# A Griffin-style layer on one core: the output projection in pairs of column groups, with seven block products for eight in some chunks

## The chip, the core and the metric

The kernel runs on one core of a Trainium2 chip. The core has a matrix engine (TensorE, PE in the profile, its weight loads PEld), a vector engine (VectorE, DVE), a scalar engine (ScalarE, ACT), GpSimd (POOL) and a queue engine (SyncE, SP) from which nearly all transfers are issued. Matmuls accumulate in PSUM, which has eight banks of 128 x 512 float32; everything else lies in SBUF. Each engine works through its own queue in order and waits on semaphores for the others. The metric is the device time of one execution in microseconds; less is better.

## The reference

One layer (DEPTH = 1), 256 tokens, width 2048, all in float32:

```python
h = rmsnorm(x, norm_mix_g);  u = h @ w_in          # 12,288 columns
# short-conv branch -> ya, recurrent branch (HGRN2, 8 heads) -> yb
m = sigmoid(ga) * (ya @ w_a_out) + sigmoid(gb) * (yb @ w_b_out)
x = x + m @ w_o                                      # the output projection
gate = sigmoid(rmsnorm(x, ple_norm_g) @ w_ple_gate)
x = x + gate * (p @ w_ple_proj)
return rmsnorm(x, final_norm_g)
```

The output projection is a product of 256 x 2048 by 2048 x 2048. Its result, added to x, is what the gate projection reads after it.

## The kernel before

**Products.** A float32 operand is split into a high part `hi`, rounded to the type that TensorE takes at full rate, and a low part `lo`, the remainder. Each product is three matmuls: hi x hi, hi x lo, lo x hi (`product`, L1097 to L1102). Activations lie transposed in SBUF, 16 row tiles k of 128 features by 256 tokens (two token halves t); they are the stationary operand, and the weights stream past in rows of 512 columns.

**Steps.** All weights pass in one list of 316 steps. A step is a chunk of 256 weight rows by 512 columns: two row tiles, two token halves, three matmuls, so twelve matmuls of 512 columns. A column group of a 2048-row matrix has eight chunks. The groups in order: the small projection PP (4), sixteen groups of the branches, the merge gates ga and gb with A (`w_a`) and B (`w_b`) for each of four column groups, four groups O (`w_o`) and four groups PG (`w_ple_gate`).

**Weights.** `load` (L103) brings two chunks, 1 MB, into one of three `raw` buffers. `split` (L130) writes hi on ScalarE (L151) and lo on VectorE (L152) into one of four `whi`/`wlo` pairs; some steps take theirs from another pool instead, among them the pool `late` from the start of PG, which takes over the memory of the pool `m`. Before each step the main loop splits ahead by three steps and more (`ahead`, L1093), so a split waits until TensorE has finished the step that held its buffer.

**Gate pairs.** For column groups 1 to 3 the gates ga and gb are computed together ("GG"). In four of the eight chunks the eight block products (2 token halves x 2 row tiles x 2 gates) are replaced by seven (the Strassen-Winograd form); the list `PAIR` gives the order of joined units ("S") and plain units of two chunks. A joined unit has four parts with 6, 3, 6 and 6 matmuls. It needs sums of weight blocks, made by VectorE in `combine_weights` (L163, L166, L167), and sums of activation blocks, made once by `forms` (L739 to L747). The products 1, 5, 6, 7 gather in four banks "s", the rest in four banks "g", and `ep_pair` (L754) puts them together on VectorE (L761).

**Epilogues.** What follows a group is a generator (`ep_...`). The main loop resumes every active one after each step, behind the splits of that step. `turned` (L283) transposes a block of 128 x 1024: four transfers of 128 KB out to DRAM (L292), one of 512 KB back in (L294), and a transposition of 32 x 32 blocks on VectorE (L298). The order on each engine's queue is then set by a scheduler, which keeps the dependencies.

**Around the change.** `ep_bb` makes a slice of m, turns it and stores its parts (L810, L811). `ep_o`, once per O group, adds the PSUM banks to x (L821), copies the sum (L822) into a tile that is turned, squares it (L829), and stores the transposed, scaled block as `x1T` (`put`, L256 and L257). Block j becomes the row tiles 4j to 4j+3 of x1T, which every PG group reads from k = 0 to 15 in chunks 0 to 7: block 0 for chunks 0 and 1, block 1 for 2 and 3, block 2 for 4 and 5, block 3 for 6 and 7. `third_part` opens the pool of the last stages and loads the first residual columns, `residual` the others, `load_gfin` the final gain.

Of the kernel before, what the change touches and what calls it, by code (L numbers as in the profile page):

```python
# [15 lines left out]
P = 128  # L16
# [7 lines left out]
CW = 512  # L24
# [17 lines left out]
PAIR = ("S", 0), (0, 2), ("S", 1), (1, 2), ("S", 4), (0, 6), ("S", 5), (1, 6)  # L42
PAIRED = [c for u, c in PAIR if u == "S"]

# [7 lines left out]
def hybrid_kernel(ctx, tc, xT, x, pT, prm, gfin, masks, w_in, w_a, w_b, w_o, w_pg, w_pp, out):  # L52
# [77 lines left out]
    def split(pos, c0=0, c1=2 * CW):  # L130
# [9 lines left out]
        if more(pos) and pos % (4 + MORE) < MORE:  # L140
            pool, n = pools["tmp2"], MORE
# [17 lines left out]
    def combine_weights(pos):  # L159

        b = load(pos).rearrange("p i (k c) -> p (i k) c", k=2)
        t2 = half[unit_of[pos]] = pools["tmp2"].tile([P, CW], F32, tag="t2", bufs=2, name=nm("t2"))
# [8 lines left out]
    for n, (kind, j) in enumerate(IN_ORDER):  # L171
        if j == 0 or kind not in ("ga", "gb"):
            groups.append((kind, j, w_in, n, "hT"))
        elif kind == "ga":
            groups.append(("GG", j, w_in, n, "hT"))
# [3 lines left out]
    groups += [("O", j, w_o, j, "mT") for j in range(4)]  # L179
# [10 lines left out]
    for gi, (kind, j, w, g, op) in enumerate(groups):  # L190
        if kind != "GG":
# [3 lines left out]
        for n, (u, c) in enumerate(PAIR):  # L195
# [3 lines left out]
    last_group = len(steps) - w_pg.shape[2]  # L199


    LEAD, MORE = 3, 1
    first_pair = min(pos for pos, s in enumerate(joint) if s)
    last_pair = max(pos for pos, s in enumerate(joint) if s)

    def more(pos):

        return first_pair - 12 <= pos <= last_pair + 8
# [511 lines left out]
    def forms():  # L720


        for n in range(0, len(PAIRED), 2):
            raw, f = t4(), t4()
            r = raw.rearrange("p (u k t) -> p u k t", u=2, k=2)
            for u in range(2):
                c = PAIRED[n + u]
                nc.sync.dma_start(out=r[:, u], in_=xT[:, 2 * c : 2 * c + 2, :])
            for u in range(2):
                yield  # L730
                for k in range(2):
                    h = r[:, u, k, :]
                    nc.scalar.activation(
                        out=h, in_=h, func=AF.Identity, scale=gain(PRM_GMIX, 2 * PAIRED[n + u] + k)
                    )
            yield
            a11, a12, a21, a22 = (r[:, :, k, t * P : (t + 1) * P] for t in range(2) for k in range(2))
            s1, s2, s3, s4 = (f[:, i * 2 * P : (i + 1) * 2 * P].rearrange("p (u t) -> p u t", u=2) for i in range(4))
            nc.vector.scalar_tensor_tensor(out=s1, in0=a21, scalar=-1.0, in1=a22, op0=ALU.mult, op1=ALU.subtract)  # L739
            nc.vector.scalar_tensor_tensor(out=s2, in0=s1, scalar=-1.0, in1=a11, op0=ALU.mult, op1=ALU.subtract)  # L740
            yield
            nc.vector.tensor_tensor(out=s3, in0=a11, in1=a21, op=ALU.subtract)
            nc.vector.tensor_tensor(out=s4, in0=a12, in1=s2, op=ALU.subtract)
            yield
            hi, lo = (pools["tmp2"].tile([P, 1024], F32R, tag="S" + x, bufs=2, name=nm("S" + x)) for x in "hl")
            nc.scalar.activation(out=hi, in_=f, func=AF.Copy)
            nc.vector.tensor_tensor(out=lo, in0=f, in1=hi.bitcast(F32), op=ALU.subtract)  # L747
            for u in range(2):
                for i in range(4):
                    s = slice((2 * i + u) * P, (2 * i + u + 1) * P)  # L750
                    state["S", PAIRED[n + u], i] = hi[:, s], lo[:, s]
# [43 lines left out]
    def ep_bb(j, psum):  # L795
# [15 lines left out]
        v = nc.vector.tensor_tensor(out=lo, in0=m, in1=hi.bitcast(F32), op=ALU.subtract)  # L811
        if j == 3:

            state["before"] = [(a.ins, v.ins), ()]

    def ep_o(j, psum):
        xs = state["x"]
        x1 = t4()
        for t in range(NT):
            d = xs[:, t, j * CW : (j + 1) * CW]  # L820
            nc.vector.tensor_tensor(out=d, in0=d, in1=psum[t], op=ALU.add)  # L821
            nc.scalar.activation(out=spread(x1, t), in_=blocks(d), func=AF.Copy)  # L822
# [119 lines left out]
    def ep_last(t, halves):  # L942
# [10 lines left out]
        "ga": ep_ga, "gb": ep_gb, "A": ep_a, "B": ep_bb, "O": ep_o, "PG": ep_pg, "PP": ep_pp,  # L953
# [139 lines left out]
    def ahead(pos):  # L1093

        return LEAD + min(max(pos - (last_group - 20), 0) // 4, 5) + MORE * (first_pair - 8 <= pos <= last_pair + 8 - MORE)
# [16 lines left out]
    def pair_products(at):  # L1112

        n, part = at
        u, c = PAIR[n]
# [3 lines left out]
        def add(name, xh, xl, s):  # L1119
            k = left[name]  # L1120
# [6 lines left out]
        def tile_of(k, t):  # L1127
            return (x[:, k, t * P : (t + 1) * P] for x in state["hT"])
# [8 lines left out]
        elif part == 1:  # L1137
            add(6, *state["S", c, 1], a)
        elif part == 2:
            add(5, *state["S", c, 0], a)  # L1140
            add((1, 0), *tile_of(2 * c + 1, 1), b)
        else:
            add((0, 1), *state["S", c, 3], a)
            add(7, *state["S", c, 2], b)
# [4 lines left out]
    plain = [4 * sum(u == i for u, _ in PAIR) for i in range(2)]  # L1149
    total = {(t, g): plain[g] + len(PAIRED) * ((t, g) != (1, 1)) for g in range(2) for t in range(NT)}  # L1150
    total.update({n: len(PAIRED) for n in (1, 5, 6, 7)})

    psum = None
    for pos, (gi, c) in enumerate(steps[:last_group]):
        kind, j, w, g, opname = groups[gi]
# [35 lines left out]
        if kind == "GG":  # L1191
            if c == (0, 0):
                left = dict(total)
                banks = {n: bank("g" if type(n) is tuple else "s") for n in total}
# [157 lines left out]
```

## Time and profile before

| what | value |
|---|---|
| time, median of 3 runs | 817.54 us (817.17 to 819.13) |
| profiled execution, its time | 816.79 us |
| its span, first to last instruction | 815.0 us |
| granted TensorE clock, mean | 0.996 |
| TensorE busy | 804.8 us (99%), 4199 matmuls recorded |
| VectorE busy | 603.9 us (74%) |
| ScalarE busy | 455.8 us (56%) |
| weight loads of w_o | 16 of 1 MB, 5.7 us each from issue to landing |

In the profile's rows of groups, `out<-in` are the program's tile names without buffer numbers, then the shape, the count, the busy time and the mean of one in ns; after the second bar stands the idle time of the engine just before them and what ended it. A timeline row is start, duration, engine, line, operation, and in brackets the idle time before it with its releaser. A row of windows gives, for one stretch, its length and then PE, PEld, DVE, ACT and POOL busy with their instruction counts, the granted clock, the DMA share and GB/s. A row of the chain of waits is start, duration and what the end of the program depended on then. Line numbers are those of the kernel before.

### The profile page before, as it was taken

The numbers are of one execution on the slowest core, as the hardware profiler recorded it, in microseconds if no ns is written. First come the engines' busy times: TensorE is split into PE (matmuls) and PEld (weight loads), VectorE is DVE, ScalarE is ACT, GpSimd is POOL, SyncE is SP. The second block draws the span as 40 slices with busy tenths as digits, with TensorE's granted clock in tenths as the row PEclk, the third lists the DMA queues.
The fourth block names the chain that finished last, engine by engine and source line by source line (L and its number), as shares of the span: only waits on it lengthen the run. The fifth ranks groups of instructions, "written<-read, shape, count | busy, mean of one in ns | idle before, by whom it ended". The sixth has DMA issues, their size and how long they took to land.

```text
span 815.0 us, 10926 instructions
## 1 busy us (share of the span) xinstructions
PE 804.8 (99%) x4199; PEld 668.8 (82%) x4200; DVE 603.9 (74%) x711; ACT 455.8 (56%) x596; POOL 91.1 (11%) x75
## 2 busy tenths in 40 slices
PE   9999999999999999999999999999999999999996
PEld 7888888888888888888888888888888888888885
DVE  6746697967766498967768998998996656679734
ACT  7666465555565465465664565554564455567522
POOL 1000045400000055200001001000100000001210
PEclk9999999999999999999999999999999999999998
DMA  9969655647767555748764774774765788887702
GB/s 341 375 267 335 231 176 205 232 158 240 255 236 249 201 178 191 225 153 262 265 232 155 236 278 142 226 272 144 252 256 170 260 296 298 285 285 280 296 1 104
DMA packets 45556, 188.32 MB, mean 231 GB/s; under 512 B 5184, under 2 KB 14656, under 8 KB 29888
## 3 DMA queue, kind: packets, MB, share of 16 engines
q1 hardware_dynamic: 45360, 187.36, 66.1%
q8 instruction: 33, 0.54, 0.3%
q10 hardware_dynamic: 144, 0.26, 0.1%
q14 instruction: 19, 0.16, 0.1%
HBM read 173.97 MB, written 13.63 MB: 230 GB/s over the span
## 4 chain that ended last, share of the span: by engine, by line
PE 93%; DVE 3%; issue 1%; DMA 1%; ACT 1%; ACTq 0%; POOLq 0%; POOL 0%
PE g L1102 80%; PE g L1122 7%; PE s L1122 3%; DVE wlo L152 2%; ACT whi L151 1%; PE s L1102 1%; PE s L448 1%; DMA raw<-in_w_a 1%; DMA raw<-in_w_pp 1%; DVE raw L163 0%; DVE t L166 0%; PE s L581 0%; PE s L604 0%; PE s L605 0%; PE s L603 0%
## 5 line engine op out<-in xcount | busy, mean ns | idle before, releaser
L152 DVE TENSOR_TENSOR wlo<-raw,whi 128x1024 fp32r<-128x1024 f32 (+1 forms) x307 | 382.5, 1262 | 168.4 <-ACT whi L151 165.3
L151 ACT ACTIVATE whi<-raw 128x1024 fp32r<-128x1024 f32 (+1 forms) x307 | 317.1, 1049 | 254.1 <-PE g L1102 205.7
L1102 PE MATMUL g<-wlo,xh 128*128 128x512 f32 (+1 forms) x720 | 276.7, 384 | 0.0
L1102 PE MATMUL g<-whi,xl 128*128 128x512 f32 (+1 forms) x720 | 276.7, 384 | 0.0
L1102 PE MATMUL g<-whi,xh 128*128 128x512 f32 (+1 forms) x720 | 276.3, 385 | 0.0
L1102 PEld LDWEIGHTS g<-whi,xl 128*128 128x128 f32 x720 | 135.3, 188 | 27.0
L1102 PEld LDWEIGHTS g<-wlo,xh 128*128 128x128 f32 x720 | 135.3, 188 | 26.8
L1102 PEld LDWEIGHTS g<-whi,xh 128*128 128x128 f32 x720 | 135.3, 188 | 26.6
L1102 PE MATMUL g<-whi,mh 128*128 128x512 f32 x128 | 49.8, 389 | 0.0
L1102 PE MATMUL g<-wlo,mh 128*128 128x512 f32 x128 | 49.8, 389 | 0.0
L1102 PE MATMUL g<-whi,ml 128*128 128x512 f32 x128 | 49.6, 389 | 0.0
L1122 PE MATMUL g<-whi,xh 128*128 128x512 f32 x120 | 46.7, 389 | 0.0
L1122 PE MATMUL g<-wlo,xh 128*128 128x512 f32 x120 | 46.7, 389 | 0.0
L1122 PE MATMUL g<-whi,xl 128*128 128x512 f32 x120 | 46.7, 389 | 0.0
L151 ACT ACTIVATE whi<-t 128x512 fp32r<-128x512 f32 x12 | 7.6, 634 | 49.5 <-DVE t L166 49.5
L804 POOL TENSOR_TENSOR t<-ga,gb 128x512 f32<-128x512 f32 x6 | 10.6, 1786 | 193.6 <-issue 118.7
L1102 PE MATMUL g<-whi,yaTh 128*128 128x512 f32 (+1 forms) x74 | 28.0, 389 | 1.1 <-ACT whi L151 0.9
L1102 PEld LDWEIGHTS g<-whi,mh 128*128 128x128 f32 x128 | 24.0, 188 | 5.0
L1102 PEld LDWEIGHTS g<-whi,ml 128*128 128x128 f32 x128 | 24.0, 188 | 5.0
L1102 PEld LDWEIGHTS g<-wlo,mh 128*128 128x128 f32 x128 | 24.0, 188 | 4.9
L502 POOL TENSOR_TENSOR t<-b 128x512 f32<-128x512 f32 x10 | 20.3, 2034 | 68.5 <-DMA t<-turn 41.0
L1102 PE MATMUL g<-wlo,yaTh 128*128 128x512 f32 (+1 forms) x74 | 28.0, 384 | 0.0
(202 smaller groups left out, 860.6 us busy)
## 6 DMA issues: line engine op xcount, KB each, us to landing
raw<-in_w_in SPq DMA_DIRECT2D x73, 1024.0 KB, 4.8
raw<-in_w_in SPq DMA_DIRECT2D x34, 512.0 KB, 6.1
raw<-in_w_o SPq DMA_DIRECT2D x16, 1024.0 KB, 5.7
raw<-in_w_pg SPq DMA_DIRECT2D x16, 1024.0 KB, 5.3
turn<-t SPq DMA_DIRECT2D x72, 128.0 KB, 2.6
t<-turn SPq DMA_DIRECT2D x18, 512.0 KB, 5.2
raw<-in_w_a SPq DMA_DIRECT2D x8, 1024.0 KB, 5.2
raw<-in_w_b SPq DMA_DIRECT2D x8, 1024.0 KB, 6.4
```

The source lines that it names most:

```text
L151: a = nc.scalar.activation(out=hi[:, s], in_=src[:, s], func=AF.Copy)
L152: v = nc.vector.tensor_tensor(out=lo[:, s], in0=src[:, s], in1=hi[:, s].bitcast(F32), op=ALU.subtract)
L448: nc.tensor.matmul(heads(bk)[r, h, c if at is None else slice(at, at + 32)], key(h)[:, r], query(h)[:, c], start=True, stop=True, tile_pos ...
L502: nc.gpsimd.tensor_tensor(out=er, in0=br, in1=ref, op=ALU.subtract)
L804: (nc.vector if j == 3 else nc.gpsimd).tensor_tensor(out=spread(m, t), in0=blocks(ga[:, s]), in1=blocks(gb[:, s]), op=ALU.add)
L1102: nc.tensor.matmul(psum, a, b, start=first and n == 0, stop=last and n == 2)
L1122: nc.tensor.matmul(banks[name], x, y[:, s], start=k == total[name] and i == 0, stop=k == 1 and i == 2)
```

## The change

The four groups O become two pairs "OO", each of two column groups, with the scheme of the gate pairs: here the two halves are two column groups of one matrix. In two of the eight chunks (0 and 1) of each pair seven block products take the place of eight. The sums of activation blocks of m are made once, at the end of `ep_bb` of the first m slice, in the second gate pair. The epilogue `ep_outs` starts when the second joined unit ends: it puts the first column group together, starts its transposition (`turned_out`), and does the second column group after the pair's last step. The lists `OUT0` and `OUT1` give the order of the units. Along with it: the temporary tiles t4 of the gate stage are three instead of four, the weight-sum tile t2 one instead of two, banks are taken at first use, the extra split buffer is also used in the later part of the pairs, and the residual and gain loads stand at other steps.

```diff
+OUT0 = (0, 2), (1, 2), (0, 4), (1, 4), ("S", 0), (0, 6), ("S", 1), (1, 6)
+OUT1 = (0, 2), (1, 2), (0, 4), ("S", 0), (1, 4), (0, 6), ("S", 1), (1, 6)
...
-        bufs = bufs or {"tmp1": 8, "tmp2": 4, "tmp3": 5}[state["tmp"]]
+        bufs = bufs or {"tmp1": 8, "tmp2": 3, "tmp3": 5}[state["tmp"]]
...
-    groups += [("O", j, w_o, j, "mT") for j in range(4)]
+    groups += [("OO", j, w_o, 2 * j, "mT", (OUT0, OUT1)[j]) for j in range(2)]
...
+    gates = range(gates[0] - 12, outs[0])
+    outs = range(outs[0] + 8, outs[-1] + 1)
...
+    def forms(op, pool, tag, r, chunks):
+        f = t4()
+        a11, a12, a21, a22 = (r[:, :, k, t * P : (t + 1) * P] for t in range(2) for k in range(2))
...
+        nc.vector.scalar_tensor_tensor(out=s1, in0=a21, scalar=-1.0, in1=a22, op0=ALU.mult, op1=ALU.subtract)
+        nc.vector.scalar_tensor_tensor(out=s2, in0=s1, scalar=-1.0, in1=a11, op0=ALU.mult, op1=ALU.subtract)
+        yield
+        nc.vector.tensor_tensor(out=s3, in0=a11, in1=a21, op=ALU.subtract)
+        nc.vector.tensor_tensor(out=s4, in0=a12, in1=s2, op=ALU.subtract)
+        yield
...
+        nc.scalar.activation(out=hi, in_=f, func=AF.Copy)
+        nc.vector.tensor_tensor(out=lo, in0=f, in1=hi.bitcast(F32), op=ALU.subtract)
...
+        if j == 0:
+            yield
+            yield from forms("mT", pools["m"], "Sm", m.rearrange("p (u k t) -> p u k t", u=2, k=2), (0, 1))
...
-    def ep_o(j, psum):
+    def ep_outs(p, e, m):
+        xs, g = state["x"], t4()
+        a, b = slice(0, CW), slice(CW, 2 * CW)
...
+        nc.scalar.activation(out=g[:, a], in_=m[1], func=AF.Copy)
+        add(x0, x0, e[0, 0])
+        add(x0, x0, g[:, a])
+        add(g[:, a], g[:, a], m[6])
+        add(g[:, b], g[:, a], m[7])
+        add(x1, x1, e[1, 0])
+        add(x1, x1, g[:, b])
+        first = turned_out(2 * p)
+        next(first)
+        active.append(first)
+        yield
+        add(both, both, m[5].rearrange("p (o c) -> p o c", o=1).to_broadcast([P, 2, CW]))
+        while not state["ended", p]:
+            yield
+        for t in range(NT):
+            add(cols(1)[:, t, :], cols(1)[:, t, :], e[t, 1])
+        add(cols(1), cols(1), both)
+        yield from turned_out(2 * p + 1)
+
+    def turned_out(j):
         xs = state["x"]
         x1 = t4()
         for t in range(NT):
-            d = xs[:, t, j * CW : (j + 1) * CW]
-            nc.vector.tensor_tensor(out=d, in0=d, in1=psum[t], op=ALU.add)
-            nc.scalar.activation(out=spread(x1, t), in_=blocks(d), func=AF.Copy)
+            nc.scalar.activation(out=spread(x1, t), in_=blocks(xs[:, t, j * CW : (j + 1) * CW]), func=AF.Copy)
         turn = turned(x1, 2)
         next(turn)
         yield
...
+            if kind == "OO" and j == 0 and c == (4, 3):
+                residual(1)
+                state["x1T"] = operand(big, "x", KT)
+            if kind == "OO" and j == 1 and c in ((0, 1), (1, 1)):
+                residual(2 + c[0])
+            if kind == "OO" and j == 1 and c == (4, 1):
+                load_gfin()
```

More of the change, by code (lines that the diff above doesn't have):

```diff
@@ L188, in add_step @@
         joint.append(s)
-    for gi, (kind, j, w, g, op) in enumerate(groups):
-        if kind != "GG":
+    for gi, (kind, j, w, g, op, *program) in enumerate(groups):
+        if not program:
             for c in range(w.shape[2]):
@@ L732, in forms @@
                     h = r[:, u, k, :]
-                    nc.scalar.activation(
-                        out=h, in_=h, func=AF.Identity, scale=gain(PRM_GMIX, 2 * PAIRED[n + u] + k)
-                    )
+                    nc.scalar.activation(out=h, in_=h, func=AF.Identity, scale=gain(PRM_GMIX, 2 * chunks[u] + k))
             yield
[L737 to L751, printed above, removed]
+            yield from forms("hT", pools["tmp2"], f"Sx{n}", r, chunks)
             yield
@@ L1093, in ahead @@
     def ahead(pos):
-        return LEAD + min(max(pos - (last_group - 20), 0) // 4, 5) + MORE * (first_pair - 8 <= pos <= last_pair + 8 - MORE)
+        return LEAD + min(max(pos - (last_group - 20), 0) // 4, 5) + MORE * (more(pos + LEAD) is not None and more(pos + LEAD + MORE) == more(pos + LEAD))
     def product(psum, op, k, t, hi, lo, first, last, which=(0, 1, 2)):
@@ L1119, in add @@
         def add(name, xh, xl, s):
+            if name not in banks:
+                banks[name] = bank("g" if type(name) is tuple else "s")
             k = left[name]
```

100 lines of the change are left out of this document (57 added, 43 removed).

## The prediction

> **What bounds the kernel now.** I read the page's engine rows first, then the windows of single stages, then the chain of waits, then timelines around the two stage borders the change touches.
>
> ```profile
> span 815.0 us, 10926 instructions
> PE 804.8 (99%) x4199; PEld 668.8 (82%) x4200; DVE 603.9 (74%) x711; ACT 455.8 (56%) x596; POOL 91.1 (11%) x75
> 506.30:547.10 40.80, 40.80 (x182) 33.78 (x181) 38.23 (x38) 24.03 (x26) 3.53 (x2) 1.00 0.72 252
> 632.00:719.00 87.00, 87.00 (x385) 72.07 (x384) 55.47 (x60) 46.07 (x63) 0.00 (x0) 1.00 0.80 280
> 479.07 5.44 PE g L1122 x24
> ```
>
> TensorE is the bound: in the output projection (third row, 87.00 us) it is busy throughout, and matmuls start every 5.44/24 = 0.2267 us, so a plain chunk step of 12 takes 2.72 us. The paired gate stage before it (506 to 547) already works with seven products; VectorE is there busy 38.23 of 40.80 us. How near VectorE is to the bound there, the chain of waits tells:
>
> ```profile
> 506.50 1.07 ACT whi L151
> 512.71 1.24 DVE raw L163
> 537.12 1.23 DVE wlo L152
> 538.37 5.10 DMA raw<-in_w_a
> 543.58 1.07 ACT whi L151
> 547.63 0.61 DVE ga L761
> 548.28 11.88 PE g L1102 x51
> ```
>
> From 506.50 to 548.24 the chain never touches TensorE: it runs over VectorE's splits and weight sums, through a weight load that a late split released, to the add that frees a PSUM bank, and TensorE's next group waits for that add. TensorE loses almost nothing, but the cushion at 548 is zero: VectorE work added to this stretch comes out at its end in full.
>
> **Removed.** Each pair of column groups has two chunks with seven products of three matmuls instead of eight: 2 x 2 x 3 = 12 matmuls x 0.2267 = 2.72 us of TensorE. All 0.33% of it is on the path. I treat 0.3%, 2.45 us, as what a measurement can tell from no change; the gain alone hardly passes that.
>
> **Added, first place: the forms of m in the second gate pair.** After the first m slice is stored, VectorE builds four sums and one split:
>
> ```profile
> L747 DVE TENSOR_TENSOR Sl<-t,Sh 128x1024 fp32r<-128x1024 f32 x2 | 2.4, 1222 | 0.0
> L739 DVE SCALAR_TENSOR_TENSOR t<-t x2: 421/421/421, 408.8 to 424.8; 128x256 f32<-128x256 f32 x2
> L742 DVE TENSOR_TENSOR t<-t x2: 418/418/419, 408.5 to 426.9; 128x256 f32<-128x256 f32 x2
> 503.62 2.49 DVE L152 TENSOR_TENSOR wlo<-raw,whi 128x1024 fp32r<-128x1024 f32 x2 [0.46 <-ACT whi L151]
> 507.60 5.08 DVE L152 TENSOR_TENSOR wlo<-raw,whi 128x1024 fp32r<-128x1024 f32 x3 [0.30 <-ACT whi L151]
> ```
>
> 2 x 0.42 + 2 x 0.42 + 1.22 = 2.9 us; instructions overlap by nearly 0.1 each, so 2.45. In the changed instruction order they stand inside the first joined chunk, the split ahead of the two multiplications (L799) that end there, so they delay the chain above. VectorE's idle time in that place is 0.46 + 0.30 = 0.76. Delay: 2.45 - 0.76 = 1.7; POOL's addition (L804), which waits for L799, is also pushed onto the next splits, and I take **1.8**. Bounds: 0 (all absorbed) and 2.9. Its ScalarE copy of 1 us is hidden beside VectorE.
>
> **Added, second place: inside the second output pair.** A joined chunk costs VectorE three and a half splits and the weight sums; each pair also gets a longer epilogue:
>
> ```profile
> L152 DVE TENSOR_TENSOR wlo<-raw,whi 128x1024 fp32r<-128x1024 f32 x302 | 379.8, 1273 | 168.2 <-ACT whi L151 165.1 <-PE g L1102 0.9 <-PE s L1102 0.9
> L163 DVE TENSOR_TENSOR raw<-raw 128x1024 f32<-128x1024 f32 x12 | 14.7, 1224 | 0.3
> L166 DVE TENSOR_TENSOR t<-raw 128x512 f32<-128x512 f32 x12 | 8.3, 693 | 0.4
> L821 DVE TENSOR_TENSOR xs<-xs,g 128x512 f32<-128x512 f32 x8 | 5.1, 682 | 0.0
> L761 DVE TENSOR_TENSOR gb<-gb,s 128x1024 f32<-128x1024 f32 x3 | 3.7, 1222 | 0.1
> ```
>
> Joined chunk: 3 x 1.27 + 0.69 + 1.22 + 2 x 0.69 = 7.1 us against 2 x 1.27 = 2.5 for the two steps it replaces: +4.6, four times 18.2. Epilogue: eight adds of 0.68 and two of 1.22 against four of 0.68: +5.2, twice 10.3. VectorE: 55.47 + 28.5 = 84.0 us, about 10% less with the overlaps, in 84.3 us of TensorE. It fits on average; order decides. Let F be the end of the first pair. The second has six plain steps (to F+16.3), a joined chunk (to F+21.1), then unit (1,4). The fourth and third parts of that chunk are split late: ScalarE's queue has the fourth first, its buffer comes free after plain step five, F+13.6; so ScalarE ends at F+15.6, VectorE at F+17.0. Behind it in VectorE's queue stands the transposition of the first output block (1.24 us, row below), then on ScalarE four scalings (1.71), only then the split of unit (1,4): ScalarE F+20.0 to 21.0, VectorE until F+22.2. TensorE wants the low half at F+21.3: wait **0.95**; bounds 0 and 2. The weights of (1,4), issued behind two "turn" transfers at about F+10, land by F+16 and are not late.
>
> **Moved, third place: the start of the gate projection PG.** Before, the third output block was transposed eight steps earlier, and only the fourth came here:
>
> ```profile
> 718.80 1.28 DVE L821 TENSOR_TENSOR xs<-xs,g 128x512 f32<-128x512 f32 x2
> 719.04 0.39 PE L1102 MATMUL g<-whi,xh 128*128 128x512 f32 x1
> 719.01 1.06 ACT L151 ACTIVATE whi<-raw 128x1024 fp32r<-128x1024 f32 x1 [1.38 <-PE g L1102]
> 721.11 0.62 ACT L822 ACTIVATE t<-xs 128x512 f32<-128x512 f32 x1
> 721.75 2.22 SPq L292 DMA_DIRECT2D turn<-t  x4
> 722.25 3.89 ACT L151 ACTIVATE whi<-raw 128x1024 fp32r<-128x1024 f32 x4
> 726.77 0.34 SPq L294 DMA_DIRECT2D t<-turn  x1
> t<-turn SPq DMA_DIRECT2D x18, 512.0 KB, 5.2
> 732.55 1.24 DVE L298 STREAM_TRANSPOSE t<-t 128x1024 f32<-128x1024 f32 x1
> 733.83 1.71 ACT L256 ACTIVATE xh<-t,prm_t 128x256 fp32r<-128x256 f32 x4 [1.50 <-DVE t L298]
> 734.82 1.66 DVE L257 SCALAR_TENSOR_TENSOR xl<-t,prm_t,xh 128x256 fp32r<-128x256 f32 x4
> ```
>
> With E = 719.04, PG's first matmul: copies done at E+2.7, turned out, back in at E+7.7, transposed at E+13.5, first scaled slice about E+15.2 (0.43 a slice). PG needs it at chunk 6, E + 6 x 2.72 = E+16.3: 1.1 us spare, 0.6 for the low part. Now the third block comes here too, and PG reads it at chunk 4, **E+10.9**. Its second copy stands on ScalarE behind the splits of PG chunks 3, 4 and 5. These write the pool that takes over m's memory, so they wait for the last output matmul, as the 719.01 row did (1.38 from PE). Three splits at 3.89/4 and the copy: E + 2.9 + 0.6 = E+3.5. From the end of the copies (721.73) to the first slice (734.26) it took 12.5, of which 0.6 was a transposition held behind a split (726.77 + 5.2 = 731.97, not 732.55): the slice is ready at E+15.4 to E+16.0. TensorE waits 4.5 to 5.1; with the low half **5.1**. Bounds: 2 (copy not held, both transfers quick) and 7. The fourth block's copies, two splits later at E+7.4, cross the third's return on SP, which is issued behind its first two parts; back out about E+12.6, landing E+18, slice E+21; chunk 6 now stands at E+16.3+5.1 = E+21.4: covered, 0.2 at most, taken as nothing.
>
> What such a wait does to the clock, no row shows; the longest wait of the trace, with the granted clock about it:
>
> ```profile
> 5.36 0.50 PE L1102 MATMUL g<-whi,yaTh 128*128 128x256 f32 x2 [0.93 <-ACT whi L151]
> PEclk9999999999999999999999999999999999999998
> ```
>
> After 0.93 us none of the slices that follow shows a lower clock (the last one is the kernel's tail). I take no loss for 5 us either. The Trainium skill, "TensorE: Matmul & The Clock Gate", section "What's actually happening", says that one wholly idle window of about 3.4 us halves the clock until as long a busy one has passed; by it, as an estimate, half of 3.4 us, 1.7 us, would come on top.
>
> **At nothing.** Later sums and bank releases: after F VectorE has one split (1.27), one wide add (1.22) and two adds (0.68 each) queued, so the last bank is free at about F+3.9, while the second unit wants it at F+5.4. The t4 ring of three, the single t2 and the earlier residual and gain loads: the reused buffers were read a unit or more before, and the loads are issued a joined chunk or more before their use. If that cover is gone, a late load costs about one transfer, the 5.2 us above.
>
> **Sum.** -2.72 + 1.8 + 0.95 + 5.1 = +5.1. The profiled execution took 816.79 (span 815.0): 821.9. The median shown, 817.54, lies 0.75 above it: **822.6**.
>
> **Rivals.** (a) The gain stands: transfers land in time, VectorE absorbs the rest. 817.54 - 2.72 = 814.8. For it: a covered fourth block today. Decisive: the third block's slice ready by E+10.9, when its copy would have to end before the last output matmul; its place in the queue, behind three splits that wait for that matmul, speaks against it. (b) Only PG waits, VectorE's delays vanish in lookahead (four to five steps): 817.54 - 2.72 + 5.1 = 819.9. (c) Only the VectorE delays: 817.54 - 2.72 + 2.75 = 817.6, if the splits of PG don't wait. (d) The long wait lowers the granted clock: were it half for as long as the wait, 5.1/2 = 2.5 more, 825.1. By the estimate from the Trainium skill's page it would be 824.3. (e) VectorE, 84.0 of 84.3, becomes the pair stage's bound: without the overlaps and with a second late unit like (1,4) some 3 us more, 825.6.
>
> **How the numbers follow.** All three waits as costed, 0.48 (821 to 824.2, slower); (d) 0.15 slower; (e) 0.06 slower; (b) 0.17, at the bound of 820.0: 0.05 slower, 0.12 same; (c) 0.08 same; (a) 0.06 faster. Slower 0.74, same 0.20, faster 0.06. The likeliest is 822.6. From 817.5 to 826.5 the range takes in (b), (d), (e) and most of (c); it leaves out (a), half of (c) and part of (e), together under 2 in 10.
>
> **What would show it.** 4187 matmuls against 4199 if records are complete; a wait of about 5 us of PE on the third slice (L256's counterpart) four steps into PG, after the copy that stands behind three splits; about 1 us at unit (1,4); the first matmul of the group after the second gate pair some 1.8 us later than the 0.3 of now; the granted clock after the long wait. Wrong it would be by ScalarE copying before E, or by PE waiting nowhere over 1 us.

## The result and the profile after

| | before | after |
|---|---|---|
| median, us | 817.18 (6 runs, 817.03 to 819.13) | 823.40 (6 runs, 822.86 to 823.59) |
| ratio | 1 | 1.0070, 95% interval 1.0057 to 1.0083 |
| profiled execution, us | 816.79 | 823.01 |
| its span, us | 815.0 | 821.1 |
| mean granted clock | 0.996 | 0.995 |

The change makes the kernel slower by 6.2 us, 0.70%. The head of the profile's page after the change:

```profile
span 821.1 us, 10969 instructions
PE 805.7 (98%) x4188; PEld 667.5 (81%) x4188; DVE 631.9 (77%) x748; ACT 462.8 (56%) x607; POOL 88.9 (11%) x75
```

The busy time of TensorE did not fall with its instructions: 11 matmuls fewer are recorded (12 are gone in the program), yet PE is busy 0.9 us longer than the 804.8 before. So some matmuls took longer; the table below has 1.6 us of that at a lower clock, and the rest stands mostly where TensorE starts up or resumes after a wait. VectorE is busy 28.0 us longer (631.9 - 603.9). The waits of TensorE after the change (engine, bank, line, what it waited for: us in total, times, longest):

```profile
PE g L1144 <- ACT xh L261: 3.8, 1, 3.8
PE g L1144 <- DVE ga L770: 0.9, 1, 0.9
...
PE g L1166 <- DVE wlo L153: 0.5, 1, 0.5
PE s L1166 <- DVE wlo L153: 0.3, 1, 0.3
```

L1144 is the plain product (L1102 before), L1166 that of the pairs. The first row is PG's start, the second is that of the third gate group, which waits for an add of the second gate pair, the third belongs to the second output pair and the fourth to the second gate pair. None is over 0.3 us in the kernel before, apart from the kernel's start. The timeline of TensorE at PG's start after the change (start, duration, engine, line, operation, idle time before it):

```profile
729.82 0.39 PE L1144 MATMUL g<-wlo,xh 128*128 128x512 f32 x1
730.04 0.39 PE L1144 MATMUL g<-whi,xl 128*128 128x512 f32 x1
734.26 0.50 PE L1144 MATMUL g<-whi,xh 128*128 128x512 f32 x1 [3.83 <-ACT xh L261]
734.60 0.40 PE L1144 MATMUL g<-wlo,xh 128*128 128x512 f32 x1
734.83 0.44 PE L1144 MATMUL g<-whi,xl 128*128 128x512 f32 x1
735.11 0.56 PE L1144 MATMUL g<-whi,xh 128*128 128x512 f32 x1
735.47 0.63 PE L1144 MATMUL g<-wlo,xh 128*128 128x512 f32 x1
735.89 0.63 PE L1144 MATMUL g<-whi,xl 128*128 128x512 f32 x1
...
738.45 0.46 PE L1144 MATMUL g<-whi,xl 128*128 128x512 f32 x1
738.75 0.39 PE L1144 MATMUL g<-whi,xh 128*128 128x512 f32 x1
```

Read the starts, not the durations: 0.227 us apart up to 730.04, then 4.22 us without a start, then from 735.11 to 738.75 nine steps of 0.40 on average (most 0.426). The row of windows for that stretch gives the length, PE's busy time with its instructions, the granted clock, the DMA share and GB/s:

```profile
735.10:738.50 3.40, 3.40 (x10) 0.51 1.02 411
```

The granted clock is 0.51 for 3.4 us: TensorE is called busy all through and does half the work. The loss is 3.64 - 9 x 0.227 = 1.60 us.

So the 6.1 us between the spans are made up like this, each item by the starts of matmuls less 0.227 a matmul:

| item | us |
|---|---|
| 12 matmuls fewer | -2.72 |
| place 1: 0.60 at 519.1 to 520.1, and 1.22 instead of 0.43 at the third gate group, 549 | +1.4 |
| place 2: unit (1,4), 697.0 to 699.0 | +1.04 |
| place 3: the third block's slice, 730.0 to 734.6 | +4.1 |
| half clock behind it | +1.6 |
| start of the execution (first product at 5.82 us, before 5.36) | +0.46 |
| rest | +0.2 |

The start varies from one execution to the next, whatever the kernel: in the traces of e3, e5, f2 and o1 below, matmuls of 512 columns stand 0.427 us apart until 9.1 to 9.4 us, so that 15 matmuls fall between 5 and 9 us instead of 20 to 22, and the products behind run about 1.5 us late. So the single times of most kernels here lie in two groups some 1.5 to 2.5 us apart, and below stretches inside the trace are compared as well, from the 100th product to the last matmul (779.7 us before, 785.4 after).

The chain of place 3, rows of the timelines of ScalarE, SP and VectorE after the change. The last output matmul starts at 719.16, PG's first, E, at 719.39:

```profile
719.36 2.96 ACT L152 ACTIVATE whi<-raw 128x1024 fp32r<-128x1024 f32 x3
722.23 0.62 ACT L864 ACTIVATE t<-xs 128x512 f32<-128x512 f32 x1
722.87 5.24 SPq L297 DMA_DIRECT2D turn<-t  x6
728.28 0.34 SPq L299 DMA_DIRECT2D t<-turn  x1
732.42 1.25 DVE L303 STREAM_TRANSPOSE t<-t 128x1024 f32<-128x1024 f32 x1 [1.62 <-DMA t<-turn]
733.70 1.71 ACT L261 ACTIVATE xh<-t,prm_t 128x256 fp32r<-128x256 f32 x4 [5.18 <-DVE t L303]
```

Three splits at E, then the second half of the third block's copy, the transfers out, the return at E+8.9 behind the first two transfers of the fourth block (the x6 instead of x4), back in after 4.1 us, transposition, first slice at 734.13 = E+14.7. PG wants it at E+10.9.

### The profile page after: what moved, and what is told of

The parts are those of the page before. It is cut to its first block, busy times and chain, and to the rows that moved or that the text cites. A ratio compares the mean times of both kernels' runs of the same rounds, so it can differ in the third digit from the quotient of the medians.

```text
span 821.1 us, 10969 instructions
## 1 busy us (share of the span) xinstructions
PE 805.7 (98%) x4188; PEld 667.5 (81%) x4188; DVE 631.9 (77%) x748; ACT 462.8 (56%) x607; POOL 88.9 (11%) x75
## 4 chain that ended last, share of the span: by engine, by line
PE 85%; DVE 8%; issue 2%; ACT 2%; DMA 2%; ACTq 0%; SPq 0%; POOLq 0%; POOL 0%; DVEq 0%
PE g L1144 66%; PE g L1166 13%; DVE wlo L153 4%; PE s L1166 3%; ACT whi L152 2%; DVE raw L164 1%; PE s L1144 1%; PE s L453 1%; DMA raw<-in_w_a 1%; DMA raw<-in_w_pp 1%; DVE xs L838 1%; DMA t<-turn 1%; DVE t L303 0%; DVE t L167 0%; ACT xh L261 0%
## 5 line engine op out<-in xcount | busy, mean ns | idle before, releaser
L1144 PE MATMUL g<-whi,xh 128*128 128x512 f32 (+1 forms) x720 | 277.4, 386 | 3.8 <-ACT xh L261 3.8
L1144 PE MATMUL g<-wlo,xh 128*128 128x512 f32 (+1 forms) x720 | 277.5, 385 | 0.0
L1144 PE MATMUL g<-whi,xl 128*128 128x512 f32 (+1 forms) x720 | 277.2, 385 | 0.0
L1144 PEld LDWEIGHTS g<-whi,xh 128*128 128x128 f32 x720 | 135.7, 188 | 31.4 <-ACT xh L261 4.2
L1144 PEld LDWEIGHTS g<-whi,xl 128*128 128x128 f32 x720 | 135.7, 189 | 27.2 <-DVE xl L262 0.2
L1144 PEld LDWEIGHTS g<-wlo,xh 128*128 128x128 f32 x720 | 135.7, 188 | 26.5
L152 ACT ACTIVATE whi<-t 128x512 fp32r<-128x512 f32 x16 | 10.1, 634 | 64.9 <-DVE t L167 64.9
L1166 PE MATMUL g<-wlo,xh 128*128 128x512 f32 x120 | 46.7, 389 | 0.0
L1166 PE MATMUL g<-whi,xl 128*128 128x512 f32 x120 | 46.7, 389 | 0.0
L1166 PE MATMUL g<-whi,xh 128*128 128x512 f32 x120 | 46.7, 389 | 0.0
L1166 PE MATMUL g<-wlo,mh 128*128 128x512 f32 x104 | 40.6, 390 | 0.5 <-DVE wlo L153 0.5
L1166 PE MATMUL g<-whi,ml 128*128 128x512 f32 x104 | 40.5, 389 | 0.0
L1166 PE MATMUL g<-whi,mh 128*128 128x512 f32 x104 | 40.1, 390 | 0.0
L1144 PE MATMUL g<-whi,yaTh 128*128 128x512 f32 (+1 forms) x74 | 28.1, 389 | 1.8 <-DVE ga L770 0.9
L1144 PE MATMUL g<-wlo,yaTh 128*128 128x512 f32 (+1 forms) x74 | 27.9, 384 | 0.0
L1144 PE MATMUL g<-whi,yaTl 128*128 128x512 f32 (+1 forms) x74 | 27.9, 384 | 0.0
L1166 PEld LDWEIGHTS g<-whi,xh 128*128 128x128 f32 x120 | 22.5, 188 | 4.7
L1166 PEld LDWEIGHTS g<-whi,xl 128*128 128x128 f32 x120 | 22.5, 188 | 4.7
```

Source lines behind the costliest of these rows:

```text
L152: a = nc.scalar.activation(out=hi[:, s], in_=src[:, s], func=AF.Copy)
L1144: nc.tensor.matmul(psum, a, b, start=first and n == 0, stop=last and n == 2)
L1166: nc.tensor.matmul(banks[name], x, y[:, s], start=k == total[name] and i == 0, stop=k == 1 and i == 2)
```

## The experiments

All times are medians; the kernel before ran beside every one on the same chip, 817.2 to 817.5.

### Each place by itself

**e3: place 1 alone.** The kernel before, with nothing but the sums of m and the buffers that pay for them:

```diff
-        bufs = bufs or {"tmp1": 8, "tmp2": 4, "tmp3": 5}[state["tmp"]]
+        bufs = bufs or {"tmp1": 8, "tmp2": 3, "tmp3": 5}[state["tmp"]]
...
-        t2 = half[unit_of[pos]] = pools["tmp2"].tile([P, CW], F32, tag="t2", bufs=2, name=nm("t2"))
+        t2 = half[unit_of[pos]] = pools["tmp2"].tile([P, CW], F32, tag="t2", bufs=1, name=nm("t2"))
...
+        if j == 0:
+            yield
...
+            nc.scalar.activation(out=shi, in_=f, func=AF.Copy)
+            nc.vector.tensor_tensor(out=slo, in0=f, in1=shi.bitcast(F32), op=ALU.subtract)
```

> The kernel before with one part of the change: the sums of m for the joined chunks are formed where the changed kernel forms them, in the second gate pair, with their work tile and the two buffers fewer that pay for it, and are used by nothing. Theory (place 1): VectorE and ScalarE are delayed there by the same instructions, and the add that frees a bank before the third gate group comes about 0.8 us later and a split 0.6 us later: 817.2 + 1.4 = 818.6 us. Rival (the loss at 519 and 549 us comes from other edits, as the order of the groups or the pools' buffers): 817.2 us, within 0.3 us, with TensorE's wait before the third gate group at 0.2 us as before.

Measured: 818.69 (11 runs), ratio 1.0016, interval 1.0007 to 1.0025; from the 100th product on 781.2 against 779.7, +1.5. TensorE's waits show the two rows of the changed kernel:

```profile
PE g L1116 <- DVE ga L761: 0.9, 1, 0.9
...
PE s L1136 <- DVE wlo L152: 0.3, 1, 0.3
```

Place 1 is real, comes with the sums of m and the buffers that pay for them, and costs 1.4 to 1.5 us.

**e4: place 1 taken away.** The changed kernel with the sums formed three calls of their generator earlier (the main loop calls it once a step):

```diff
-        m = yield from turned(m, 2 if j == 3 else 19)
+        m = yield from turned(m, {0: 16, 3: 2}.get(j, 19))
```

> The changed kernel with one number other: the first block of m waits for 16 calls before its transposition and not for 19, so that the sums of m are formed earlier than in the last joined chunk of the second gate pair. Theory (place 1 is a matter of where the 2.45 us of VectorE stand): the loss of 1.4 us at 519 and 549 us falls to that of the kernel before, 0.3; 823.4 - 1.4 = 822.0 us, places 2 and 3 as they were. Rival (VectorE is full there wherever they stand): 823.4 us.

Measured: 822.93 (6 runs, 821.23 to 824.31), where 822.0 was expected; ratio 1.0060, interval 1.0044 to 1.0076. The trace is the clearer witness: 784.1 us from the 100th product on instead of 785.4, neither of the two waits of place 1 is left in TensorE's list, and the largest gap between starts there is back to 0.49 us (0.54 before the change, 1.34 in the changed kernel). Places 2 and 3 stand as in the changed kernel. The buffers are still the fewer ones, so the cost hung on where the 2.45 us of VectorE stood, and one number removes it.

**e5: place 2.** One number again, the first block's transposition behind the split of unit (1,4):

```diff
-        turn = turned(x1, 2)
+        turn = turned(x1, 9 if j == 0 else 2)
```

> The changed kernel with one number other: the first block's transposition in the second output pair's place waits for nine calls instead of two, so that the split of unit (1, 4) is issued to VectorE ahead of it. Theory (place 2): TensorE's wait of 0.5 us at 698.6 us and the gaps beside it, 1.04 us in all, go; 823.4 - 1.0 = 822.4 us. Rival (the split is late for its weights or for VectorE's other work there, not for its place in the queue): the wait stays and the time is 823.4 us; a split delayed elsewhere by the transposition in its new place would make it 823.4 us too, with the wait at another unit.

Measured: 826.40, ratio 1.0100, interval 1.0085 to 1.0116: 3.0 us slower than the changed kernel, where 1.0 us less was expected, and from the 100th product on as well (788.4). The wait at 698.6 is gone, and two things come in its place. First, 1.1 us are lost at the next joined chunk (a gap of 0.95 us between starts at 711.35), behind ScalarE's splits:

```profile
709.72 1.06 ACT L152 ACTIVATE whi<-raw 128x1024 fp32r<-128x1024 f32 x1 [3.46 <-PE g L1166]
710.68 0.61 ACT L152 ACTIVATE whi<-t 128x512 fp32r<-128x512 f32 x1
```

The split of the weight sum (`whi<-t`), which in the changed kernel goes first, now stands behind one that waits for TensorE to free its buffer; VectorE has no work for 1.02 us just then and is not what is full. Second, place 3 grows. SP's rows:

```profile
725.14 6.65 SPq L297 DMA_DIRECT2D turn<-t  x6
731.97 0.34 SPq L299 DMA_DIRECT2D t<-turn  x1
```

The third block's return again stands behind two transfers of the fourth block, whose copies now end at 731.0. TensorE waits 6.1 us, and then runs at a granted clock of 0.50 for 5.2 us.

**h1: half of the change.** Only the first two column groups are a pair; the last two are plain groups with the plain epilogue:

```diff
-    groups += [("OO", j, w_o, 2 * j, "mT", (OUT0, OUT1)[j]) for j in range(2)]
+    groups += [("OO", 0, w_o, 0, "mT", OUT0)] + [("O", j, w_o, j, "mT") for j in (2, 3)]
...
```

> Half of the change: only the first two column groups of the output projection are a pair with two joined chunks, the last two are plain groups as before, with the plain epilogue. Theory (the gain is 0.227 us a matmul wherever it is made, and places 2 and 3 belong to the second pair): 6 matmuls fewer, -1.36 us; place 1 stays, since the sums of m are formed at the same point, +1.4; no wait of 0.5 us at a split in the third group and none of 3.8 us in PG, so 817.2 - 1.36 + 1.4 = 817.2 us. Rival (a joined pair costs VectorE and the queues so much that the losses of places 2 and 3 come with each pair): 817.2 - 1.36 + 1.4 and half of the 6.7 us of places 2 and 3 and of the low clock, 820.6 us.

Measured: 817.08 (12 runs), ratio 0.9995, interval 0.9985 to 1.0004, where 817.2 was expected: 6 matmuls won, place 1 lost, nothing at places 2 and 3. The first joined pair carries no price on TensorE beyond place 1; the losses at places 2 and 3 come with the second one.

**h2: the half, and place 1 taken away** (the edits of h1 and e4 together).

> The half of the change with the first pair alone, and the sums of m formed earlier: the first block of m waits for 16 calls before its transposition and not for 19, so that the sums stand in the group before the second gate pair's end and not in its last joined chunk. Theory: place 1 goes, 817.2 - 1.36 = 815.9 us, faster than the kernel before, with TensorE's wait before the third gate group at 0.2 us again. Rival (VectorE is full all through the second gate pair and pays the 2.45 us of the sums wherever they stand): 817.2 us, with the wait at the third gate group near 0.9 us.

Measured: 815.45 (12 runs), ratio 0.9973, interval 0.9964 to 0.9983: faster than before. TensorE's waits hold nothing over 0.3 us but the kernel's start:

```profile
PE s L1028 <- PEq L1405: 0.8, 1, 0.8
PE g L1150 <- ACT whi L152: 0.3, 1, 0.3
PE g L1150 <- DVE ga L770: 0.2, 1, 0.2
```

### The clock

**e2: the wait filled.** Ahead of PG's fifth step (`n` = 16):

```diff
+        if kind == "PG" and j == 0 and c == 4:
+            wb = bank("s")
+            ones = [nc.const_aps.tensor(1.0, [P, i], mybir.dt.bfloat16) for i in (P, CW)]
+            for _ in range(n):
+                tc.keep_in_program_order(nc.tensor.matmul(wb, *ones, start=True, stop=True))
```

> The changed kernel with 16 products of constant tiles, 128x128 by 128x512, ahead of the fifth chunk of PG's first group, into a bank that is then not read: they only fill the wait of 3.8 us on the slice. Theory (the half clock after the wait comes from TensorE's having stood idle for about 4 us): the wait of the fifth chunk's first matmul ends at the same time, since ScalarE ends it, but the matmuls behind it stand 0.227 us apart and not 0.427 us, granted clock 0.99 or more; 823.4 - 1.55 = 821.9 us. Rival (the wide spacing from 735.1 to 738.5 us is the supply of operands after the wait, or belongs to the phase): the spacing stays and the time is 823.4 us.

Measured: 821.38, ratio 1.0054, interval 1.0040 to 1.0067. From the 100th product on it is 784.1 us against 785.4. TensorE resumes at the same moment, and the matmuls behind stand 0.227 us apart:

```profile
730.17 3.67 PE L1273 MATMUL s<-const-bfloat16-1.0 128*128 128x512 bf16 x16
734.26 0.50 PE L1144 MATMUL g<-whi,xh 128*128 128x512 f32 x1 [0.42 <-ACT xh L261]
...
735.34 0.39 PE L1144 MATMUL g<-wlo,xh 128*128 128x512 f32 x1
735.57 0.40 PE L1144 MATMUL g<-whi,xl 128*128 128x512 f32 x1
```

The wide spacing after the wait is the idle time's doing, not the operands'.

**d6: a part of the wait filled** (the same edit, `n` = 6).

> The changed kernel with 6 products of constant tiles in the place where e2 had 16: they fill 1.4 us of the wait of 4.0 us and leave TensorE idle for about 2.6 us in one piece. Theory (what lowers the clock is a stretch in which TensorE does nothing for more than about 3 us; a wait of 1.8 us in f2 did not, those of 4.0 us did): no low clock, matmuls 0.227 us apart after the wait, 823.4 - 1.55 = 821.9 us, as e2. Rival (the clock follows the share of idle time in a longer stretch, and e2 held it only because it filled nearly all of the wait): 0.427 us apart as in the changed kernel for part or all of 3.4 us, 822.6 to 823.4 us.

Measured: 823.85 (4 runs), ratio 1.0076, interval 1.0061 to 1.0092: no gain. My threshold fell:

```profile
730.09 1.48 PE L1273 MATMUL s<-const-bfloat16-1.0 128*128 128x512 bf16 x6
734.17 0.50 PE L1144 MATMUL g<-whi,xh 128*128 128x512 f32 x1 [2.60 <-ACT xh L261]
...
735.45 0.63 PE L1144 MATMUL g<-wlo,xh 128*128 128x512 f32 x1
735.88 0.63 PE L1144 MATMUL g<-whi,xl 128*128 128x512 f32 x1
```

The rival held. 2.60 us without work in one piece were enough, and the half clock (granted 0.50) lasts 3.4 us, as after 3.83 us of idling.

### Place 3: what holds the third block

**f4: its copies ahead of the splits.**

```diff
+            cp = nc.scalar.activation(out=spread(x1, t), in_=blocks(xs[:, t, j * CW : (j + 1) * CW]), func=AF.Copy)
+        if j == 2:
+            state["before"] = [(cp.ins,)]
```

> The changed kernel with one edit: the third block's copies go ahead of the splits of PG that are issued after them; the order of the second output pair and the fourth block stay. Theory (the third block is late for its place behind splits, and when it comes in time the fourth is late next): the wait in PG's fifth step falls from 3.8 to between 1 and 2 us, too short for the low clock, and the fourth block, whose slice was ready 20 us after the last output matmul and is wanted at 16.3 plus that wait, makes up to 2.3 us in the seventh step: 823.4 - 4.1 - 1.55 + 1.5 + 2.3 = 821.5 us. Rival (the copy was ready to go no earlier, because VectorE's sums end only when the splits do): the wait stays at 3.8 us with the low clock behind it, 823.4 us.

Measured: 823.79, ratio 1.0071, interval 1.0058 to 1.0083. That is the rival's time, but not the rival's reason. Rows of ScalarE, SP and VectorE:

```profile
719.55 0.63 ACT L864 ACTIVATE t<-xs 128x512 f32<-128x512 f32 x1 [1.61 <-DVE xs L838]
728.16 1.16 ACT L864 ACTIVATE t<-xs 128x512 f32<-128x512 f32 x2 [2.00 <-DVE xs L838]
730.45 1.99 ACT L152 ACTIVATE whi<-raw 128x1024 fp32r<-128x1024 f32 x2
733.94 1.71 ACT L261 ACTIVATE xh<-t,prm_t 128x256 fp32r<-128x256 f32 x4 [1.50 <-DVE t L303]
...
724.95 0.34 SPq L299 DMA_DIRECT2D t<-turn  x1
...
731.52 1.23 DVE L153 TENSOR_TENSOR wlo<-raw,whi 128x1024 fp32r<-128x1024 f32 x1 [0.58 <-ACT whi L152]
732.67 1.24 DVE L303 STREAM_TRANSPOSE t<-t 128x1024 f32<-128x1024 f32 x1
```

The copy did go 2.7 us earlier and the return 3.3 us earlier. The transposition starts when it did before (732.67; 732.42 in the changed kernel), and nothing in its row waits for a transfer: it stands in VectorE's queue behind a split, that split waits for ScalarE's at 730.45, and this one stands behind the fourth block's copies at 728.16. One hold was taken away, and a second that ended at the same time lay under it.

**f2: copies of both blocks ahead, and the second joined chunk two steps earlier.**

```diff
-OUT1 = (0, 2), (1, 2), (0, 4), ("S", 0), (1, 4), (0, 6), ("S", 1), (1, 6)
+OUT1 = (0, 2), (1, 2), (0, 4), ("S", 0), (0, 6), ("S", 1), (1, 4), (1, 6)
...
+        if j >= 2:
+            state["before"] = [(cp.ins,)]
```

> The changed kernel with two edits for the start of PG: the copies of the third and fourth blocks go ahead of the splits of PG on ScalarE, and the second joined chunk of the second output pair ends two steps earlier, so that the sums of the third block start earlier. Theory (place 3 and the clock behind it are what PG's start costs): the wait of 3.8 us on ScalarE's slice in the fifth step of PG goes, and with it the 3.4 us at a granted clock of 0.51, so 823.4 - 4.1 - 1.55 = 817.8 us, with no long wait of TensorE and a granted clock of 0.99 or more from step one of PG on. Rival one (the chain from the copy over the round trip to memory to the slice is too long however early the copy is): a wait of over 2 us stays and the time is 821 us or more. Rival two (the low clock belongs to the phase and not to the wait): the wait goes and 1.5 us at 0.51 stay, 819.3 us.

Measured: 823.93 (822.3 to 824.1), ratio 1.0074, interval 1.0061 to 1.0086. As expected, no wait for a slice is left and the granted clock is 1.00 all through PG's start. But the 5.7 us are nearly all spent elsewhere:

```profile
PE g L1146 <- DVE wlo L153: 2.0, 2, 1.4
PE s L1168 <- ACT whi L152: 1.2, 1, 1.2
...
PE g L1146 <- ACT whi L152: 0.7, 2, 0.5
```

By the gaps between starts, 2.4 us go at the second joined chunk, which now follows the first after two steps, its weight sums late; 3.0 us go in PG at splits that stand behind the fourth block's copies and the transposition. My theory named a wait to remove and not what was next in the same queues.

**p1 and p5: the order on SP.** The third block's return ahead of all transfers of the fourth; p1 is the changed kernel with it, p5 is e5 with it:

```diff
-        nc.sync.dma_start(out=src, in_=d.rearrange("p a x -> p (a x)"))
+        state["back"] = nc.sync.dma_start(out=src, in_=d.rearrange("p a x -> p (a x)")).ins
...
-        next(turn)
+        with ExitStack() as order:
+            if j == 3:
+                order.enter_context(tc.issue_after(state["back"]))
+            next(turn)
```

> The changed kernel with one order fixed on SP: the transfer that brings the third block back is issued ahead of all four that take the fourth block out, where it stands behind the first two of them (issued at 728.28 us; the third block's last way out was issued at 725.14 and such a transfer lands 2.1 to 2.7 us after its issue). Theory (the place in SP's queue is a part of place 3): the return is issued 0.4 to 1.0 us earlier and the wait of 3.8 us falls to about 3.1; 823.4 - 0.7 = 822.7 us, or 821.1 us if so short a wait leaves the clock alone. Rival (the return waits for its own data only): 823.4 us.

> The kernel e5 (transposition of the first block later, place 2 gone, but a wait of 6.1 us in PG) with the same order fixed on SP. There the return of the third block was issued at 731.97 us, behind two transfers of the fourth block whose copies ended at 731.0, though the third block's own last way out must have landed by about 729.7. Theory: e5 lost at place 3 what it won at place 2 because of SP's queue; the return is issued about 2.2 us earlier, the wait falls to about 3.9 us and the low clock after it from 4.3 us to 3.4 or less: 824.3 (e5 with the early start) - 2.2 - 0.4 = 821.7 us, under the changed kernel. Rival (the longer wait of e5 comes from its copies and splits, which stand later): the wait stays near 6 us and the time at 824.3 us or more.

Measured: p1 821.26, ratio 1.0047, interval 1.0034 to 1.0059; p5 822.21, ratio 1.0059, interval 1.0045 to 1.0072. From the 100th product on p5 gains 5.1 us on e5 (788.4 to 783.3), and its return is issued at 727.55 instead of 731.97. p1 gains 0.8 us there on the changed kernel (785.4 to 784.6), where the medians say 2.1 with intervals that touch. The reason is not SP alone, and in p1 not SP at all: there the return is issued no earlier than in the changed kernel (728.28), though all four transfers of the fourth block now stand behind it:

```profile
728.30 0.34 SPq L299 DMA_DIRECT2D t<-turn  x1
```

So p1's time, near the 821.1 expected, does not support its theory. With the new dependency the scheduler also changed TensorE's own queue. In the instruction order of p1 and p5, six matmuls of PG's second group stand ahead of the first group's fifth step and 24 more ahead of its seventh; in the changed kernel none and six. TensorE in p1 waits for a split of that other group, and no more for the slice:

```profile
732.70 0.73 PE L1147 MATMUL g<-whi,xh 128*128 128x512 f32 x2 [2.43 <-ACT whi L152]
733.96 0.80 PE L1147 MATMUL g<-wlo,xh 128*128 128x512 f32 x1 [0.53 <-DVE wlo L153]
```

How much of either gain is SP's order and how much TensorE's, these two runs do not separate. They pointed to the cure, though: other work for TensorE.

**o1: all of the change, place 1 taken away, and the first two groups of PG alternating by halves.**

```diff
+        if kind == "PG" and j < 2:
+            for h in range(2 * (j == 0)):
+                for q in range(2):
+                    for c in range(4 * h, 4 * h + 4):
+                        add_step(gi + q, c, w, g + q, c, len(steps) % 2, False)
+            continue
...
-            psum = [bank("s" if kind == "PP" and j > 1 else "g") for _ in range(NT)]
+            psums[gi] = [bank("s" if kind == "PP" and j > 1 else "g") for _ in range(NT)]
+        psum = psums[gi]
```

(and the edit of e4)

> The changed kernel, both pairs, with two edits: the sums of m are formed earlier (16 calls and not 19, as in e4), and the steps of the first two groups of PG alternate by halves: four steps of the first, four of the second, then the other four of each. The third block is then wanted 16 x 0.68 = 10.9 us later, 21.8 us after the last output matmul, and the fourth at 27.2, against the 15 and 20 us at which their slices were ready. Theory (three separate places and the clock behind the third): place 1 falls to the 0.3 us of the kernel before, place 3 and the low clock go, place 2 stays; 817.2 - 2.72 + 1.04 + 0.2 = 815.7 us, faster than the kernel before, with no wait of TensorE above 1 us in PG. Rival (the splits, weight loads and transfers of PG's start are too many for ScalarE, VectorE and SP in whatever order, so that TensorE waits for a split instead, as in f2): a wait of 2 us or more stays in PG and the time is 817.5 us or more.

Measured: 815.43 (7 runs), ratio 0.9969, interval 0.9958 to 0.9981, where 815.7 was expected. TensorE works through PG's start without a gap at full clock (window of 32 us: length, PE busy, clock, DMA share, GB/s), and of the waits of the three places only place 2 is left (second row). The third block comes no earlier: its first slice is ready at 734.39 (third row, 0.43 a slice), as in the changed kernel, but TensorE has other work until about 741:

```profile
718.00:750.00 32.00, 32.00 (x143) 1.00 0.84 292
PE g L1172 <- DVE wlo L153: 0.5, 1, 0.5
733.96 1.71 ACT L267 ACTIVATE xh<-t,prm_t 128x256 fp32r<-128x256 f32 x4 [5.33 <-DVE t L309]
```

In the changed kernel the same window has 28.17 us busy and 117 matmuls at 0.95. From the 100th product on it is 778.3 us against 779.7 before: -1.4, where -2.72 + 1.04 would be -1.7. It is level with h2 (815.45), and both are faster than the kernel before and the changed one.

## Why the prediction was right, and where it was not

- **The time.** Forecast 822.6, measured 823.4, 0.8 us more; slower by 0.70%. Against the spans, where it worked from, it said +5.1 and the trace has +6.1.
- **The gain**: -2.72, and it is there. h1 has half of it and, with place 1 gone in h2, the trace from the 100th product on is 1.2 us shorter than before (1.36 expected); o1 has all of it.
- **Place 1**, 1.8: the mechanism is shown by e3 and e4, the size is 1.4. The prediction put the whole at the add before the third gate group. There it is 0.8 (1.22 less the 0.43 of before); 0.6 more are lost thirty microseconds earlier, at a split behind the sums, which the prediction passed over.
- **Place 2**, 0.95: measured 1.04, at the unit named and on the split named. That the transposition ahead of it is why this unit pays is shown by e5; that the loss goes with the order is not, since in e5 1.1 us are lost at the next joined chunk in its place.
- **Place 3**, 5.1: measured 4.1. The copy was timed right (E+3.5 forecast, 722.85 - 719.39 = 3.46 measured), and the slice came at E+14.7 and not at E+15.4 to 16.0, because the return landed after 4.1 us where the prediction put the median of 5.2. The step that failed is in its causes. The prediction called the copy's place behind three splits decisive. f4 took that place away and the slice came no earlier, for the transposition's place in VectorE's queue held it as long; f2 cleared both and lost the time at splits. The first slices of the third and fourth blocks come 14.7 and 20.1 us after E, and PG's first group alone has work for 10.9 and 16.3 us before it needs them: that was the cause. o1, which has 21.8 and 27.2, removes the wait while the third slice comes as late as ever.
- **The clock**, taken as nothing: mis-sized by 1.6 us. The row from which no loss was concluded had a wait of 0.93 us, which is no evidence for one of 5. Rival (d) was right about the mechanism and too high in size (2.5). The estimate worked out from the Trainium skill, "TensorE: Matmul & The Clock Gate", section "What's actually happening", was 1.7 us, and 1.60 were measured, with the clock low for 3.4 us as it says. e2 shows that the idle time is the cause. How much of it was needed is in the last section.
- **Luck in the sum.** The two errors at places 1 and 3 (0.4 and 1.0 too much) and the one at the clock (1.6 too little) cancel. With the places sized right and the clock still at nothing, the forecast would have been about 821.2, 2.2 us under the measured time.
- **The other rivals.** (a) and (c): fell with the wait of 3.8 us. (b): fell with e3. (e): in the output pairs VectorE was forecast at 84.0 us of 84.3 before overlaps; the trace has 72.3 of 84.0 (634.2 to 718.2). It did not become the bound, though in f2, where the second joined chunk comes two steps sooner, ScalarE waits for its weight sums.
- **Fourth block**, taken as covered: right as the kernel stood, since the wait for the third gave it time, as the prediction said. Where f2 removed that wait, the fourth block's copies became a hold.

## What to carry to other kernels

Work that ends a stage costs nothing until the next stage's first reader comes due; when an edit makes a second block of results late at such a border, count the whole round trip of each block against the work that the next stage can do without it, and if it does not fit, give TensorE other work there (here: half of the next group) rather than rearranging queues, where each hold removed (e5, f4, f2) uncovered the next one. Price a wait of TensorE of some 2.4 us and more with the half clock behind it, not only with its length. And 2.5 us of vector work put into a stretch without slack can cost more than half of its length, while three steps earlier it costs next to nothing: try the position before giving up the edit.

## What the runs showed of the hardware

- **How little idling halves the clock.** 2.60 us in one piece (d6) brought the half clock for 3.4 us as did 3.83 us (the changed kernel), and so did 2.43 us with 0.53 us shortly behind (p1). Waits of 1.4 us and 0.5 us in f2 and of up to 1.5 us in p5 left it at 1.00. I had expected a limit of about 3 us. The Trainium skill, "TensorE: Matmul & The Clock Gate", section "What's actually happening", speaks of an idle window of about 3.4 us; a wholly idle window of that length was not needed in d6, p1 or the changed kernel.
- **The granted clock changes on a fixed grid.** In all traces here its stretches between two changes are whole multiples of 3.413 us: the low ones last 3.41 us (6.83 in e5), the full one before the drop 730.45 us in the changed kernel, 214 times that. By these traces what decides is how long TensorE idled within one such 3.41 us, and not the length of one wait. Four rows of windows, with length, PE busy, clock, DMA share and GB/s: the changed kernel's last window ahead of the drop and the low one behind it; the drop with the least idling, at the end of the matmuls of h2; and the most idling without a drop, at the end of those of e2:

```profile
731.77:735.18 3.41, 0.92 (x4) 1.00 1.06 417
735.18:738.60 3.42, 3.42 (x10) 0.50 1.02 416
804.34:807.76 3.42, 1.46 (x13) 1.00 0.00 0
809.87:813.28 3.41, 1.54 (x13) 1.00 0.00 0
```

In the 14 traces every window at full clock in which TensorE idled 1.96 us or more was followed by the half clock (2.49 in the changed kernel, 2.54 in p1, 2.56 in d6), and none in which it idled 1.87 us or less was. The ends of matmuls are modelled in these rows, so the two figures are not exact. By them a wait of 2.4 us that two windows share evenly would leave the clock alone; no run has one.
- **The half clock can start late.** It starts at the end of the window, not of the wait: 0.92 us after TensorE has resumed in the changed kernel and 0.85 us in d6, so that the first matmuls after a wait look sound and the loss shows only in the ones that follow. In e5, after 6.1 us of idling, it is there from the first matmul on.
- **A dependency on SP moved TensorE's order** (p1, p5). This is the scheduler's doing and not the chip's, but it means that an experiment on one queue has to be read with the order of all the others beside it.
